# SwiGLU on two inner tiles at a time, and normed tiles kept in place

## The chip, the cores and the metric

The kernel runs on one core of one Trainium2 chip. The metric is device time of one execution in microseconds (us); the time of a kernel is the median of its runs. A profile comes from one further execution, whose span is taken from its first to its last instruction.

## What is computed

A decoder trunk of two layers for one sequence of 256 positions and 1024 features. Each layer has three sub-layers: a SwiGLU channel mixer (FFN), a sequence mixer (layer 0: a gated linear recurrence beside chunked linear attention; layer 1: latent attention), and a second FFN. Every sub-layer is modulated by a conditioning vector and closed by a norm over residual and output:

```python
D_MODEL = 1024; SEQ = 256; DEPTH = 2; D_FF = 2816

def layer_norm(x, g, b):
    xf = x.astype(F32)
    mu = jnp.mean(xf, -1, keepdims=True)
    var = jnp.mean(jnp.square(xf - mu), -1, keepdims=True)
    return ((xf - mu) * lax.rsqrt(var + LN_EPS) * g + b).astype(x.dtype)

def modulate(x, shift, scale):
    return x * (1 + scale[:, None, :]) + shift[:, None, :]

def deepnorm_residual(x, f, gate, g, b, weight=1.0):
    return layer_norm(DN_ALPHA * x + weight * (1 + gate[:, None, :]) * f, g, b)

def swiglu(u, w_in, w_out):
    gate, up = jnp.split(u @ w_in, 2, axis=-1)
    return (jax.nn.silu(gate) * up) @ w_out
```

## The kernel before, in words

**Layout.** Features lie on the 128 partitions, positions along the row: x is 8 tiles (k, or f on the output side) of 128x256. The inner width of an FFN is 22 tiles (j), each with a gate half and an up half.

**Weights.** All weights stream through in slabs of 16 tiles of 128x128 by one DMA each (SyncE's queue). Half a slab, 128x1024, is split at a time into a rounded high part (ScalarE, `whi`, L338) and the rest (VectorE, `wlo`, L339). `Stream.next` keeps three half slabs converted ahead, in four buffers. Now and then a conversion is followed on VectorE by one or two reductions of modulation weights (`junk`, L388).

**Products.** Values are held as a high and a low part as well. Each product of a 128x128 weight tile is three matmuls of 256 columns (`mm3`): high by high (L407), high weight by low value (L408), low weight by high value (L409).

**The FFN** (`ffn`). The first one, which starts while the modulation vectors are still being reduced, takes 8 inner tiles for k 0 to 3 and puts the sums aside (L725), then 8 others for all k, then the first 8 for k 4 to 7, with the sums added (L731). The other three have one early tile and a group of four. What is left is taken tile by tile (the tail). `glu` handles one inner tile: Silu of the gate on ScalarE (`sg`, L429), product with the up half on VectorE (`h`, L702), and the split into `hhi` (ScalarE, L444) and `hlo` (VectorE, L445). In a group the gate and the up half of one tile share a PSUM bank; in the tail each has a bank of its own.

**The boundary** (`Boundary`). `tile_out` adds an output tile to the residual `ax`, giving `y`; `stats` forms the mean and the variance with matmuls; `center` (L603) subtracts the mean tile by tile; `rsqrt2` yields `r` (L686, L687), which is minus twice the reciprocal deviation. While this goes on, TensorE multiplies the first tiles of the next sub-layer with values that are not yet normed (`early`), and two steps on VectorE correct the results (L641, L642). `u(k)` then makes the next input's tile k: `ut` = y times a column times r (VectorE, L657), `uhi` = ut plus a column, rounded (ScalarE, L658), `ulo` = the rest (VectorE, L659). `residual` makes `ax` for the next output: `xh` = y times a column times r (VectorE, L665), then ScalarE (L666) adds a column. There are six boundaries: the last ends the kernel; the one into the odd mixer (attention) has no `u` of its own but a residual; the other four have both. In the text they are counted from the first.

**Order.** Nothing is ordered by hand but the few steps around the statistics (`manual_schedule`). A list scheduler places each engine's instructions by priority (`high_priority`, with offsets UOFF for `u`, GOFF and GLATE for `glu`, EOFF for the early values). Once placed, each engine takes its list in order, so a step that waits holds up all that stand behind it.

Of the kernel before, what the change touches and what calls it, by code (L numbers as in the profile page):

```python
# [231 lines left out]
def trunk_kernel(ctx: ExitStack, tc: tile.TileContext, xT, cvec, pos, wst, modw, colsd,  # L232
# [281 lines left out]
    class Boundary:  # L514
# [79 lines left out]
        def stats(self, y, ysq):  # L594
# [7 lines left out]
            def center(k):  # L602
                vec.tensor_tensor(self.y[:, k, :], self.y[:, k, :], mean, SUB)  # L603

            odd_next = not self.last and self.next[1] == 1 and self.next[0] % 2
            with tc.high_priority(), tc.manual_schedule(engines={DVE, ACT}):
# [8 lines left out]
                for k in range(PRE):  # L615
                    center(k)
                r, rlast = rsqrt2(v, SEQ)
                self.r = r
                if self.last:
                    for k in range(KD):  # L620
                        self.normal(k, r)
                        if k + PRE < LPOOL:
                            center(k + PRE)
                    return
# [3 lines left out]
            self.center = center  # L628
# [15 lines left out]
            if odd_next:  # L644
                for k in range(PRE, KD):
                    center(k)

        def u(self, k):
# [4 lines left out]
            with tc.high_priority(offset=UOFF):  # L653
                if k >= PRE:
                    self.center(k)
                xa = T(wk, [P, SEQ], tag="ut")
                vec.scalar_tensor_tensor(xa, self.y[:, k, :], self.hA[:, k:k + 1], self.r, MULT, MULT)  # L657
                act.activation(uhi[:, k, :], xa, AF.Identity, bias=self.B[:, k:k + 1])  # L658
                vec.scalar_tensor_tensor(ulo[:, k, :], xa, self.B[:, k:k + 1], uhi[:, k, :].bitcast(F32), ADD, SUB)  # L659

        def residual(self, ks=range(KD)):
            W.pause = False
            for k in ks:
                xg = T(wk, [P, SEQ], tag="xh", bufs=3)
                vec.scalar_tensor_tensor(xg, self.y[:, k, :], self.ag[:, k:k + 1], self.r, MULT, MULT)  # L665
                act.activation(ax[:, k, :], xg, AF.Identity, bias=self.ab[:, k:k + 1])  # L666
# [24 lines left out]
    def ffn(l, i, prev):  # L691
        with tc.tile_pool(name=nm("ffn"), bufs=1) as fp:
# [4 lines left out]
            def glu(j, pg, pu, bg=0.0, bu=0.0, off=100):  # L697
                with tc.high_priority(offset=off):
                    sg = T(wk, [P, SEQ], tag="sg")
                    ta(sg, pg, AF.Silu, bias=bg)  # L700
                    h = T(wk, [P, SEQ], tag="h")
                    vec.scalar_tensor_tensor(h, pu, bu, sg, ADD, MULT)  # L702
                    split(h, hhi[:, j, :], hlo[:, j, :])

            for j in range(EARLY if prev else 0):
                (pg, bg), (pu, bu) = prev.values[2 * j:2 * j + 2]
                glu(j, pg, pu, bg, bu)

            passes = ffn_passes(l, i)
            part = {}  # L710
            for g, ks in passes:
                grp = {j: mmps() if q < 6 else axps() for q, j in enumerate(g)}
                for k in ks:
                    prev.u(k) if prev else first_u(k)
                    for j in g:
                        for half in range(2):
                            mm3(grp[j][:, half * SEQ:(half + 1) * SEQ], W.next((m, k, half * NJ + j)), u(k),
                                k == ks[0] and half == 0, k == ks[-1], True)
# [597 lines left out]
```

## Time and profile before

| | us |
|---|---|
| median of three runs | 1040.61 (1040.7, 1035.38, 1040.61) |
| profiled execution | 1033.83 |
| its span | 1032.1 |
| DVE busy, subtraction L339 alone | 416.7 |
| ACT busy, copy L338 alone | 357.6 |

The mean granted TensorE clock of the profiled execution was 0.996. PE is TensorE's matmuls, DVE VectorE, ACT ScalarE. A row of a group gives line, engine, operation, output and inputs with their shapes and the count, then busy us and mean ns, then idle time just before and what ended it. A row of a timeline gives start, duration and the operation, and in brackets the idle time before it and what ended that. Instructions of one engine overlap a little: the time that one holds up the queue is the distance to the next start.

### The profile page before, as it was taken

The numbers are of one execution on the slowest core, as the hardware profiler recorded it, in microseconds if no ns is written. First come the engines' busy times: TensorE is split into PE (matmuls) and PEld (weight loads), VectorE is DVE, ScalarE is ACT, GpSimd is POOL, SyncE is SP. The second block draws the span as 40 slices with busy tenths as digits, with TensorE's granted clock in tenths as the row PEclk, the third lists the DMA queues.
The fourth block names the chain that finished last, engine by engine and source line by source line (L and its number), as shares of the span: only waits on it lengthen the run. The fifth ranks groups of instructions, "written<-read, shape, count | busy, mean of one in ns | idle before, by whom it ended". The sixth has DMA issues, their size and how long they took to land.

```text
span 1032.1 us, 20703 instructions
## 1 busy us (share of the span) xinstructions
PE 995.5 (96%) x8338; PEld 972.8 (94%) x8338; DVE 884.7 (86%) x1491; ACT 612.5 (59%) x1023; POOL 54.8 (5%) x72
## 2 busy tenths in 40 slices
PE   6999999999999989999999999999999999999995
PEld 5999999998899979999999999999998889999995
DVE  5789999797998989999998899998888799666664
ACT  4746654567886656745545665455559666545543
POOL 0000010000001020000030000002000200000200
PEclk9999999999999999999999999999999999999998
DMA  9998798554466943699977469898743146665621
GB/s 342 366 339 319 257 368 309 208 204 169 170 264 242 350 185 142 245 361 373 365 279 286 166 251 371 322 359 321 286 167 129 73 164 245 246 224 187 243 83 41
DMA packets 38578, 258.57 MB, mean 251 GB/s; under 512 B 4289, under 2 KB 6849, under 8 KB 7762
## 3 DMA queue, kind: packets, MB, share of 16 engines
q1 hardware_dynamic: 38482, 257.25, 66.7%
q8 instruction: 65, 1.06, 0.4%
q14 instruction: 31, 0.25, 0.1%
HBM read 256.18 MB, written 1.05 MB: 249 GB/s over the span
## 4 chain that ended last, share of the span: by engine, by line
PE 82%; DVE 11%; issue 2%; ACT 2%; DMA 2%; POOL 0%; SPq 0%; DVEq 0%; ACTq 0%
PE mm L409 25%; PE mm L407 25%; PE mm L408 25%; DVE wlo L339 4%; DVE junk L388 2%; DMA wraw<-modw 1%; ACT whi L338 1%; DVE flat L557 1%; DVE yy L581 1%; PE ax L408 1%; PE ax L407 1%; PE ax L409 1%; DVE acc L589 1%; DVE flat L731 0%; DMA rgt<-rgw 0%
## 5 line engine op out<-in xcount | busy, mean ns | idle before, releaser
L339 DVE TENSOR_TENSOR wlo<-wraw,whi 128x1024 fp32r<-128x1024 f32 x340 | 416.7, 1233 | 81.3 <-ACT whi L338 80.8
L338 ACT ACTIVATE whi<-wraw 128x1024 fp32r<-128x1024 f32 x340 | 357.6, 1058 | 212.4 <-PE mm L408 138.0
L407 PE MATMUL mm<-uhi,whi 128*128 128x256 f32 x1672 | 461.4, 278 | 11.5 <-ACT uhi L444 6.0
L409 PE MATMUL mm<-uhi,wlo 128*128 128x256 f32 x1672 | 460.1, 277 | 3.6 <-DVE wlo L339 3.6
L408 PE MATMUL mm<-ulo,whi 128*128 128x256 f32 x1672 | 462.1, 277 | 0.7 <-DVE ulo L445 0.6
L407 PEld LDWEIGHTS mm<-uhi,whi 128*128 128x128 f32 x1672 | 313.6, 188 | 14.9 <-ACT uhi L444 7.9
L409 PEld LDWEIGHTS mm<-uhi,wlo 128*128 128x128 f32 x1672 | 313.8, 188 | 4.2 <-DVE wlo L339 4.1
L408 PEld LDWEIGHTS mm<-ulo,whi 128*128 128x128 f32 x1672 | 314.8, 188 | 1.5 <-DVE ulo L445 1.2
L409 PE MATMUL mm<-hhi,wlo 128*128 128x256 f32 x704 | 194.6, 276 | 1.9 <-DVE wlo L339 1.9
L408 PE MATMUL mm<-hlo,whi 128*128 128x256 f32 x704 | 194.4, 276 | 0.0
L407 PE MATMUL mm<-hhi,whi 128*128 128x256 f32 x704 | 194.3, 276 | 0.0
L388 DVE CUSTOM_DVE_ANT_0 junk<-wraw,cact,cols 128x1024 bf16<-128x1024 f32 x144 | 184.9, 1284 | 5.7 <-DMA wraw<-modw 5.0
L409 PEld LDWEIGHTS mm<-hhi,wlo 128*128 128x128 f32 x704 | 132.1, 188 | 2.3 <-DVE wlo L339 2.3
L407 PEld LDWEIGHTS mm<-hhi,whi 128*128 128x128 f32 x704 | 132.2, 188 | 0.0
L408 PEld LDWEIGHTS mm<-hlo,whi 128*128 128x128 f32 x704 | 132.2, 188 | 0.0
L571 POOL TENSOR_TENSOR ax<-ax,shift 128x256 f32<-128x256 f32 x42 | 42.2, 1039 | 734.7 <-ACT shift L569 734.7
L444 ACT ACTIVATE hhi<-h 128x256 fp32r<-128x256 f32 x88 | 35.9, 413 | 44.3 <-DVE h L702 43.2
L585 ACT ACTIVATE ysq<-yy 128x256 f32<-128x256 f32 x42 | 17.4, 414 | 51.8 <-DVE yy L581 50.0
L702 DVE SCALAR_TENSOR_TENSOR h<-mm,sg 128x256 f32<-128x256 f32 x75 | 30.9, 418 | 7.9 <-PE mm L409 7.9
L581 DVE SCALAR_TENSOR_TENSOR yy<-mm,gate,ax 128x256 f32<-128x256 f32 x48 | 22.8, 478 | 16.2 <-PE mm L409 15.0
L445 DVE TENSOR_TENSOR hlo<-h,hhi 128x256 fp32r<-128x256 f32 x88 | 36.0, 417 | 0.0
L429 ACT ACTIVATE sg<-mm 128x256 f32<-128x256 f32 x75 | 27.4, 366 | 3.0 <-DVE h L702 1.7
(288 smaller groups left out, 1088.1 us busy)
## 6 DMA issues: line engine op xcount, KB each, us to landing
wraw<-wst SPq DMA_DIRECT2D x169, 1024.0 KB, 5.8
wraw<-modw SPq DMA_DIRECT2D x71, 1024.0 KB, 6.5
wraw<-modw SPq DMA_DIRECT2D x2, 512.0 KB, 5.4
yy<-xT SPq DMA_DIRECT2D x8, 128.0 KB, 6.8
wraw<-wst SPq DMA_DIRECT2D x2, 512.0 KB, 7.9
rgt<-rgw SPq DMA_DIRECT2D x8, 128.0 KB, 3.7
outT<-yy SPq DMA_DIRECT2D x3, 256.0 KB, 2.6
outT<-yy SPq DMA_DIRECT2D x2, 128.0 KB, 2.6
```

The source lines that it names most:

```text
L338: act.activation(hi, raw, AF.Copy)
L339: i = vec.tensor_tensor(lo, raw, hi.bitcast(F32), SUB)
L388: i = vec.tensor_tensor_reduce(junk, t, cact, 1.0, col("mod_b", (l * NMOD + v) * KD + j), MULT, ADD, self.modcols[(l, v)][:, j:j + 1])
L407: pe.matmul(ps, hi, mh, start=start, stop=False, skip_group_check=shared)
L408: pe.matmul(ps, hi, ml, start=False, stop=False, skip_group_check=shared)
L409: pe.matmul(ps, lo, mh, start=False, stop=stop, skip_group_check=shared)
L429: i = act.activation(out, in_, func, **kw)
L444: act.activation(hi, src, AF.Copy)
L445: vec.tensor_tensor(lo, src, hi.bitcast(F32), SUB)
L571: pool.tensor_tensor(ax[:, j, :], ax[:, j, :], shift, SUB)
L581: vec.scalar_tensor_tensor(y, ps, self.gate[:, f:f + 1], ax[:, f, :], MULT, ADD)
L702: vec.scalar_tensor_tensor(h, pu, bu, sg, ADD, MULT)
```

## The change

It has four parts.

1. `glu` takes two inner tiles at once: the gates of a pair share one PSUM bank, the ups another, and Silu, product, rounding and subtraction run on 128x512. There are 41 pairs; the early tile and, in the three later FFNs, the last tile stay single. The product of a pair is a tensor_tensor. The order of the weight tiles, and so the matmuls' number and weights, stays.
2. `center` works on two tiles at a time, with the mean repeated by a broadcast, at all boundaries but the last.
3. A new step `normed` multiplies two tiles at a time by `r`, in place, so that `y` then holds the normed value. `u(k)` is made from it: `uhi` and the same value unrounded, `xa`, are both made on ScalarE (scale and bias as columns), and VectorE subtracts them (`ulo`, now a tensor_tensor). The first VectorE step of `u` is gone.
4. `residual` is one ScalarE step from the same normed value; its VectorE step is gone.

The new lines in the changed kernel: center L607, normed L610, mean copy L617, v L621, the early steps L652 and L653, uhi L673, xa L674, ulo L675, residual L680, rsqrt2 L701 and L702, the products of `glu` L719 (single) and L721 (pair), the added sums L759.

```diff
+            def wide(t, n):
+                return t[:, None, :].broadcast_to([P, n, SEQ])
+            def center(k, n=2):
+                vec.tensor_tensor(self.y[:, k:k + n, :], self.y[:, k:k + n, :], wide(mean, n), SUB)
+            def normed(k, n=2):
+                vec.tensor_tensor(self.y[:, k:k + n, :], self.y[:, k:k + n, :], wide(self.r, n), MULT)
...
             if odd_next:
-                for k in range(PRE, KD):
-                    center(k)
+                for k in range(0, KD, 2):
+                    if k >= PRE:
+                        center(k)
+                    normed(k)
...
             with tc.high_priority(offset=UOFF):
-                if k >= PRE:
-                    self.center(k)
+                if k % 2 == 0:
+                    if k >= PRE:
+                        self.center(k)
+                    self.normed(k)
+                z, a, b = self.y[:, k, :], self.hA[:, k:k + 1], self.B[:, k:k + 1]
                 xa = T(wk, [P, SEQ], tag="ut")
-                vec.scalar_tensor_tensor(xa, self.y[:, k, :], self.hA[:, k:k + 1], self.r, MULT, MULT)
-                act.activation(uhi[:, k, :], xa, AF.Identity, bias=self.B[:, k:k + 1])
-                vec.scalar_tensor_tensor(ulo[:, k, :], xa, self.B[:, k:k + 1], uhi[:, k, :].bitcast(F32), ADD, SUB)
+                act.activation(uhi[:, k, :], z, AF.Identity, bias=b, scale=a)
+                act.activation(xa, z, AF.Identity, bias=b, scale=a)
+                vec.tensor_tensor(ulo[:, k, :], xa, uhi[:, k, :].bitcast(F32), SUB)
...
-                xg = T(wk, [P, SEQ], tag="xh", bufs=3)
-                vec.scalar_tensor_tensor(xg, self.y[:, k, :], self.ag[:, k:k + 1], self.r, MULT, MULT)
-                act.activation(ax[:, k, :], xg, AF.Identity, bias=self.ab[:, k:k + 1])
+                act.activation(ax[:, k, :], self.y[:, k, :], AF.Identity, bias=self.ab[:, k:k + 1],
+                               scale=self.ag[:, k:k + 1])
...
-            def glu(j, pg, pu, bg=0.0, bu=0.0, off=100):
+            def glu(j, n, pg, pu, bg=0.0, bu=0.0, off=100):
                 with tc.high_priority(offset=off):
-                    sg = T(wk, [P, SEQ], tag="sg")
+                    sg = T(wk, [P, 2 * SEQ], tag="sg")[:, :n * SEQ]
                     ta(sg, pg, AF.Silu, bias=bg)
-                    h = T(wk, [P, SEQ], tag="h")
-                    vec.scalar_tensor_tensor(h, pu, bu, sg, ADD, MULT)
-                    split(h, hhi[:, j, :], hlo[:, j, :])
+                    h = T(wk, [P, 2 * SEQ], tag="h")[:, :n * SEQ]
+                    if n == 1:
+                        vec.scalar_tensor_tensor(h, pu, bu, sg, ADD, MULT)
+                    else:
+                        vec.tensor_tensor(h, pu, sg, MULT)
+                    split(h, *(t[:, j:j + n, :].rearrange("p j s -> p (j s)") for t in (hhi, hlo)))
...
-            for j in range(max(g.stop for g, _ in passes), NJ):
+            j = max(g.stop for g, _ in passes)
+            while j < NJ:
+                n = min(2, NJ - j)
                 pp = [mmps(), mmps()]
-                for half in range(2):
-                    for k in range(KD):
-                        mm3(pp[half][:, :SEQ], W.next((m, k, half * NJ + j)), u(k),
-                            k == 0, k == KD - 1)
-                glu(j, pp[0][:, :SEQ], pp[1][:, :SEQ])
+                for q in range(n):
+                    for half in range(2):
+                        for k in range(KD):
+                            mm3(pp[half][:, q * SEQ:(q + 1) * SEQ], W.next((m, k, half * NJ + j + q)), u(k),
+                                k == 0 and q == 0, k == KD - 1, True)
+                glu(j, n, *(ps[:, :n * SEQ] for ps in pp))
+                j += n
```

How the lists of the engines come out, at three places.

VectorE in the first FFN, where the last pass's products and the first tail products are split; `mod0` rows belong to the reduction before them. Before, between two conversions:

```order
L339 TENSOR_TENSOR wlo_248_1472<-wraw_202_1216,whi_247_1471 128x1024
L702 SCALAR_TENSOR_TENSOR h_227_1360<-flat1_90_464,sg_226_1358 128x256
L702 SCALAR_TENSOR_TENSOR h_240_1433<-mm_229_1365,sg_239_1431 128x256
L388 ISA junk_249_1475,mod0_3_236_1402<-wraw_201_1214,cact_5_96,cols_6_97 128x1024
L388 ISA mod0_3_236_1402 128x1
L445 TENSOR_TENSOR hlo_31_145<-h_240_1433,hhi_30_144 128x256
L445 TENSOR_TENSOR hlo_31_145<-h_227_1360,hhi_30_144 128x256
L702 SCALAR_TENSOR_TENSOR h_252_1505<-mm_242_1438,sg_251_1503 128x256
L388 ISA junk_250_1477,mod0_3_236_1402<-wraw_201_1214,cact_5_96,cols_6_97 128x1024
L388 ISA mod0_3_236_1402 128x1
L702 SCALAR_TENSOR_TENSOR h_261_1571<-mm_254_1510,sg_260_1569 128x256
L445 TENSOR_TENSOR hlo_31_145<-h_252_1505,hhi_30_144 128x256
```

And now, at the same place:

```order
L339 TENSOR_TENSOR wlo_224_1384<-wraw_186_1128,whi_223_1383 128x1024
L388 ISA junk_222_1357,mod0_3_220_1354<-wraw_185_1126,cact_5_96,cols_6_97 128x1024
L388 ISA mod0_3_220_1354 128x1
L721 TENSOR_TENSOR h_211_1312<-flat1_90_464,sg_210_1310 128x512
L721 TENSOR_TENSOR h_232_1449<-mm_213_1317,sg_231_1447 128x512
L339 TENSOR_TENSOR wlo_228_1416<-wraw_194_1192,whi_227_1415 128x1024
L445 TENSOR_TENSOR hlo_31_145<-h_232_1449,hhi_30_144 128x512
L445 TENSOR_TENSOR hlo_31_145<-h_211_1312,hhi_30_144 128x512
L388 ISA junk_229_1419,mod0_3_220_1354<-wraw_193_1190,cact_5_96,cols_6_97 128x1024
L388 ISA mod0_3_220_1354 128x1
L339 TENSOR_TENSOR wlo_236_1456<-wraw_194_1192,whi_235_1455 128x1024
```

Four products and three splits became two and two of double width, and the two reductions no longer stand in one stretch between conversions.

VectorE in the even mixer, where the recurrence (`ya`, L843 to L853, with L853 the scans) and the attention's decays (`bc`, `lb`) are formed. Before:

```order
L665 SCALAR_TENSOR_TENSOR xh_513_3248<-yy_299_1821,ag_314_1849,r_401_2597 128x256
L968 TENSOR_TENSOR lb_457_2980<-lb_457_2980,mm_514_3251 128x256
L843 SCALAR_TENSOR_TENSOR ya1_495_3168<-xh_512_3228,ya1_495_3168 128x256
L665 SCALAR_TENSOR_TENSOR xh_517_3282<-yy_299_1821,ag_314_1849,r_401_2597 128x256
L844 TENSOR_SCALAR ya2_496_3169<-ya2_496_3169 128x1024
L665 SCALAR_TENSOR_TENSOR xh_523_3320<-yy_299_1821,ag_314_1849,r_401_2597 128x256
L845 SCALAR_TENSOR_TENSOR ya2_496_3169<-ya1_495_3168,ya2_496_3169 128x1024
L967 TENSOR_TENSOR bc_458_2981<-bc_458_2981,mm_518_3285 128x256
L846 SCALAR_TENSOR_TENSOR ya2_496_3169<-ya2_496_3169 128x1024
L339 TENSOR_TENSOR wlo_522_3291<-wraw_480_3075,whi_521_3290 128x1024
```

And now, with lines higher by 32:

```order
L1000 TENSOR_TENSOR lb_429_2908<-lb_429_2908,mm_485_3177 128x256
L875 SCALAR_TENSOR_TENSOR ya1_467_3096<-xh_484_3156,ya1_467_3096 128x256
L876 TENSOR_SCALAR ya2_468_3097<-ya2_468_3097 128x1024
L877 SCALAR_TENSOR_TENSOR ya2_468_3097<-ya1_467_3096,ya2_468_3097 128x1024
L999 TENSOR_TENSOR bc_430_2909<-bc_430_2909,mm_488_3209 128x256
L878 SCALAR_TENSOR_TENSOR ya2_468_3097<-ya2_468_3097 128x1024
L339 TENSOR_TENSOR wlo_492_3215<-wraw_452_3003,whi_491_3214 128x1024
```

The three steps of the residual are gone from between the others, whose order is kept.

The third boundary, between layer 0's second FFN and layer 1's first, on VectorE. Before, from `r` on:

```order
L687 SCALAR_TENSOR_TENSOR r_1143_7301<-t_1144_7302,r_1143_7301 128x256
L339 TENSOR_TENSOR wlo_1149_7317<-wraw_1119_7089,whi_1148_7316 128x1024
L657 SCALAR_TENSOR_TENSOR ut_1145_7309<-yy_1042_6526,hA_1048_6537,r_1143_7301 128x256
L641 SCALAR_TENSOR_TENSOR early_1151_7346<-mean_1142_7294,wab_1150_7344,mm_1146_7313 128x256
L657 SCALAR_TENSOR_TENSOR ut_1170_7431<-yy_1042_6526,hA_1048_6537,r_1143_7301 128x256
L659 SCALAR_TENSOR_TENSOR ulo_18_124<-ut_1145_7309,B_1045_6529,uhi_17_123 128x256
L642 SCALAR_TENSOR_TENSOR early_1151_7346<-early_1151_7346,r_1143_7301 128x256
```

And now:

```order
L702 SCALAR_TENSOR_TENSOR r_1063_7119<-t_1064_7120,r_1063_7119 128x256
L339 TENSOR_TENSOR wlo_1069_7136<-wraw_1039_6909,whi_1068_7135 128x1024
L610 TENSOR_TENSOR yy_962_6346<-yy_962_6346,r_1063_7119 128x512
L652 SCALAR_TENSOR_TENSOR early_1071_7165<-mean_1062_7114,wab_1070_7163,mm_1066_7132 128x256
L610 TENSOR_TENSOR yy_962_6346<-yy_962_6346,r_1063_7119 128x512
L653 SCALAR_TENSOR_TENSOR early_1071_7165<-early_1071_7165,r_1063_7119 128x256
L675 TENSOR_TENSOR ulo_18_124<-ut_1065_7128,uhi_17_123 128x256
```

Two normed pairs stand where two single steps stood, and both early steps now come ahead of the first `ulo`. The same place on ScalarE, before:

```order
L658 ACTIVATE uhi_17_123<-ut_1145_7309,B_1045_6529 128x256
L338 ACTIVATE whi_1168_7403<-wraw_1126_7155 128x1024
L429 ACTIVATE sg_1160_7389<-early_1151_7346,wab_1150_7344 128x256
L658 ACTIVATE uhi_17_123<-ut_1170_7431,B_1045_6529 128x256
L639 ACTIVATE wab_1155_7378<-mm_1152_7349 128x2
```

And now:

```order
L673 ACTIVATE uhi_17_123<-yy_962_6346,B_965_6349,hA_968_6357 128x256
L674 ACTIVATE ut_1065_7128<-yy_962_6346,B_965_6349,hA_968_6357 128x256
L673 ACTIVATE uhi_17_123<-yy_962_6346,B_965_6349,hA_968_6357 128x256
L429 ACTIVATE sg_1080_7208<-early_1071_7165,wab_1070_7163 128x256
L674 ACTIVATE ut_1090_7250<-yy_962_6346,B_965_6349,hA_968_6357 128x256
L650 ACTIVATE wab_1075_7197<-mm_1072_7168 128x2
L673 ACTIVATE uhi_17_123<-yy_962_6346,B_965_6349,hA_968_6357 128x256
L674 ACTIVATE ut_1093_7283<-yy_962_6346,B_965_6349,hA_968_6357 128x256
L673 ACTIVATE uhi_17_123<-yy_962_6346,B_965_6349,hA_968_6357 128x256
L674 ACTIVATE ut_1098_7319<-yy_962_6346,B_965_6349,hA_968_6357 128x256
L338 ACTIVATE whi_1088_7222<-wraw_1046_6975 128x1024
```

The weight copy that followed the first `uhi` now follows the fourth.

More of the change, by code (lines that the diff above doesn't have):

```diff
@@ L614, in stats @@
                 vec.tensor_tensor(v, e2, v, SUB)
-                for k in range(PRE):
-                    center(k)
+                if self.last:
+                    for k in range(PRE):
+                        center(k, 1)
+                else:
+                    for k in range(0, PRE, 2):
+                        center(k)
                 r, rlast = rsqrt2(v, SEQ)
@@ L622, in stats @@
                         if k + PRE < LPOOL:
[L623 removed]
+                            center(k + PRE, 1)
                     return
@@ L627, in stats @@
                 W.pause = PAUSE
-            self.center = center
+            self.center, self.normed = center, normed
             if not odd_next:
```

43 lines of the change are left out of this document (25 added, 18 removed).

## Prediction

> **What bounds the kernel now.** I read the page's first part, then the windows, then the waits of the matmul queue, and then the timeline around each of those waits.
>
> ```profile
> span 1032.1 us, 20703 instructions
> PE 995.5 (96%) x8338; PEld 972.8 (94%) x8338; DVE 884.7 (86%) x1491; ACT 612.5 (59%) x1023; POOL 54.8 (5%) x72
> ```
>
> TensorE is busy for 96% of the span. The change leaves its matmuls and the weight tiles as they are, so nothing can be won but in the 4% where it waits. Stretches of 20 us (columns: PE, PEld, DVE, ACT, POOL, each busy us with its count) show where VectorE is the fuller of the two:
>
> ```profile
> 100.00:120.00 20.00, 20.00 (x179) 20.00 (x178) 20.00 (x36) 13.55 (x25) 0.00 (x0) 1.00 0.74 275
> 120.00:140.00 20.00, 18.96 (x167) 18.76 (x166) 20.00 (x33) 12.46 (x20) 0.00 (x0) 1.00 0.90 333
> 260.00:280.00 20.00, 17.48 (x149) 17.04 (x148) 19.63 (x30) 16.61 (x28) 2.40 (x1) 1.00 0.43 158
> 583.00:605.00 22.00, 22.00 (x196) 22.00 (x195) 21.96 (x40) 13.66 (x23) 0.00 (x0) 1.00 0.51 186
> ```
>
> 179 matmuls in 20 us are one per 0.112 us, the undisturbed pace. In the first row VectorE has no gap at all, and TensorE still runs at full pace on the slabs converted ahead; in the second and third VectorE is as full and TensorE loses time. The waits of the matmul queue (us in all, times, longest):
>
> ```profile
> PE mm L409 <- DVE wlo L339: 6.5, 6, 1.5
> ...
> PE mm L408 <- DVE ulo L445: 0.6, 1, 0.6
> PE mm L1167 <- DVE e L1159: 0.5, 1, 0.5
> ```
>
> So of 36 us without a matmul only 6.5 + 0.6 + 0.5 = 7.6 us end on VectorE work that this change makes lighter or shifts. The list has no wait for a PSUM bank. That 7.6 us is the most that the change can give.
>
> **The change part by part.** Durations of the groups that it touches, or that resemble the new ones:
>
> ```profile
> L445 DVE TENSOR_TENSOR hlo<-h,hhi 128x256 fp32r<-128x256 f32 x88 | 36.0, 417 | 0.0
> L665 DVE SCALAR_TENSOR_TENSOR xh<-yy,ag,r 128x256 f32<-128x256 f32 x40 | 17.9, 475 | 0.0
> L657 DVE SCALAR_TENSOR_TENSOR ut<-yy,hA,r 128x256 f32<-128x256 f32 x32 | 15.2, 476 | 0.0
> L731 DVE TENSOR_TENSOR flat<-mm,flat 128x512 f32<-128x512 f32 x6 | 4.0, 681 | 0.0
> L658 ACT ACTIVATE uhi<-ut,B 128x256 fp32r<-128x256 f32 x32 | 16.0, 505 | 9.3 <-DVE ut L657 8.9
> L509 ACT ACTIVATE ut<-yy,mod,scp 128x256 f32<-128x256 f32 x8 | 4.8, 599 | 18.2 <-DVE scp L507 18.2
> ```
>
> Alone, a 128x512 operation takes 681 ns against 2 x 417 = 834, so a merge saves 153 ns. In a queue that is never empty neighbours overlap, and the start of the next row counts. Such a stretch, in the first FFN's tail, on VectorE, and the matmul that it holds up:
>
> ```profile
> 117.11 0.42 DVE L445 TENSOR_TENSOR hlo<-h,hhi 128x256 fp32r<-128x256 f32 x1
> 117.45 0.68 DVE L731 TENSOR_TENSOR flat<-ax,flat 128x512 f32<-128x512 f32 x1
> 118.05 1.21 DVE L339 TENSOR_TENSOR wlo<-wraw,whi 128x1024 fp32r<-128x1024 f32 x1
> ...
> 119.85 1.27 DVE L388 CUSTOM_DVE_ANT_0 junk<-wraw,cact,cols 128x1024 bf16<-128x1024 f32 x1
> ...
> 122.06 1.27 DVE L388 CUSTOM_DVE_ANT_0 junk<-wraw,cact,cols 128x1024 bf16<-128x1024 f32 x1
> ...
> 123.93 1.22 DVE L339 TENSOR_TENSOR wlo<-wraw,whi 128x1024 fp32r<-128x1024 f32 x1
> ```
> ```profile
> 125.20 0.38 PE L409 MATMUL mm<-uhi,wlo 128*128 128x256 f32 x1 [1.04 <-DVE wlo L339]
> ```
>
> From 117.11 to 117.45 a 256-wide operation holds the queue 0.34 us, from 117.45 to 118.05 a 512-wide one 0.60: a merge in a full queue saves 0.07 us.
>
> *Product and split, pairs, first FFN.* Eleven pairs merge 22 operations on VectorE: 22 x 0.07 = 1.5 us of relief over 90 us, which by itself moves little. The Trainium skill ("VectorE: DVE Perf Modes", section "The TRN2 errata — SBUF-src ops pay a fixed extra latency per instruction") gives an fp32 tensor_tensor (N+151)/0.96 ns and advises tiles of 512 elements and more, since the fixed part is paid once; that is 157 ns a merge and an estimated 3.5 us here, which would make the sum below 2.0 us lower. The single rows agree with it to a few ns (153 against 157), the queued rows do not. What counts more is the order. Before, two reductions, four products and three splits stand between the subtraction at 118.05 and the one at 123.93, which ends 1.04 us late for the matmul at 125.20. In the changed order one reduction, two double products or two double splits stand between neighbouring subtractions, so the late one comes over a microsecond earlier: -1.2 us (1.04, and the slower pace of the matmul after it). The two later waits of this stretch stay: the reductions before them are as many. Bounds: 0, and -2.9 us, what the stage's three waits amount to:
>
> ```profile
> PE mm L409 <- DVE wlo L339: 2.9, 3, 1.2
> ```
>
> *Residual without VectorE.* Forty L665 go (17.9 us), each 0.40 us in a full queue. They are worth time only where TensorE waits behind them, and this is the even mixer, VectorE first, then TensorE:
>
> ```profile
> 262.18 0.48 DVE L665 SCALAR_TENSOR_TENSOR xh<-yy,ag,r 128x256 f32<-128x256 f32 x1
> ...
> 270.56 3.31 DVE L339 TENSOR_TENSOR wlo<-wraw,whi 128x1024 fp32r<-128x1024 f32 x1
> ...
> 276.79 0.47 DVE L665 SCALAR_TENSOR_TENSOR xh<-yy,ag,r 128x256 f32<-128x256 f32 x1
> 277.18 1.21 DVE L339 TENSOR_TENSOR wlo<-wraw,whi 128x1024 fp32r<-128x1024 f32 x1
> ```
> ```profile
> 273.93 0.38 PE L409 MATMUL mm<-uhi,wlo 128*128 128x256 f32 x1 [1.02 <-DVE wlo L339]
> ...
> 278.45 0.38 PE L409 MATMUL mm<-uhi,wlo 128*128 128x256 f32 x1 [1.50 <-DVE wlo L339]
> ```
>
> Three L665 stand ahead of the first late subtraction and a fourth ahead of the second (277.18 - 276.79 = 0.39 each), in a queue that hardly pauses from 258 on. The first comes 1.2 us earlier and its wait of 1.02 us goes; the second comes 1.6 us earlier, but TensorE is there 1.2 us earlier too, and 0.4 us of its 1.50 goes: -1.6 us. Bounds: 0 (if the queue then waits for the scan's inputs) and -2.5, both waits. In the odd mixer one L665 and a subtraction stand ahead of the softmax products for which L1167 waits 0.5 us: -0.4 us, bounds 0 and -0.5. The scaling moves to ScalarE, 599 ns instead of 505; no matmul waits for the residual until the next sub-layer's output.
>
> *The next input at a boundary.* This is where the change adds. Third boundary, VectorE, ScalarE and TensorE in turn:
>
> ```profile
> 580.66 0.42 DVE L687 SCALAR_TENSOR_TENSOR r<-t,r 128x256 f32<-128x256 f32 x1
> 581.00 1.22 DVE L339 TENSOR_TENSOR wlo<-wraw,whi 128x1024 fp32r<-128x1024 f32 x1
> 582.13 0.48 DVE L657 SCALAR_TENSOR_TENSOR ut<-yy,hA,r 128x256 f32<-128x256 f32 x1
> ...
> 583.32 0.48 DVE L659 SCALAR_TENSOR_TENSOR ulo<-ut,B,uhi 128x256 fp32r<-128x256 f32 x1
> ```
> ```profile
> 582.65 0.51 ACT L658 ACTIVATE uhi<-ut,B 128x256 fp32r<-128x256 f32 x1 [0.47 <-DVE ut L657]
> 583.81 1.06 ACT L338 ACTIVATE whi<-wraw 128x1024 fp32r<-128x1024 f32 x1 [0.66 <-PE mm L408]
> ```
> ```profile
> 583.73 0.64 PE L407 MATMUL mm<-uhi,whi 128*128 128x256 f32 x4
> 584.21 0.28 PE L408 MATMUL mm<-ulo,whi 128*128 128x256 f32 x1
> ```
>
> Before, ulo of the first k is ready at 583.80 and first read at 584.21: 0.41 us to spare. After, r is 0.14 us later (the last mean-subtraction between t and r is a pair, 0.60 for 0.34; the two pairs ahead of t pay back 0.14 of that). Then subtraction L339, normed pair 0 from 582.27, the early value 582.87, normed pair 1 583.26, the other early step 583.86, ulo 584.19 to 584.60. Both activations are done by then (uhi 582.95 to 583.55, xa to 584.1). TensorE starts its first four L407 on time, then misses ulo by 0.4 to 0.5 us. I take 0.45 at three boundaries, which are alike. At the second, before, ulo stands ahead of a subtraction:
>
> ```profile
> 401.39 0.48 DVE L659 SCALAR_TENSOR_TENSOR ulo<-ut,B,uhi 128x256 fp32r<-128x256 f32 x1
> 401.79 1.22 DVE L339 TENSOR_TENSOR wlo<-wraw,whi 128x1024 fp32r<-128x1024 f32 x1
> ```
> ```profile
> 401.92 0.39 PE L408 MATMUL mm<-ulo,whi 128*128 128x256 f32 x1
> ```
>
> In the changed order the normed pair (0.60 for 0.40) and the subtraction (1.13 to the next start) come first, two other steps no longer do (L657 of the second k, 0.40); ulo begins about 0.93 us later, at 402.32, ends at 402.74, and the matmul of 401.92 is 0.9 us late. Cost: 3 x 0.45 + 0.9 = +2.25 us. Bounds: +1.4 (r not later, so 0.25 each and 0.7), and +4.5 (1.13 each, if a subtraction stands ahead everywhere). The fourth boundary, into the odd mixer, has neither uhi nor ulo and costs nothing.
>
> What waits behind the new work: on ScalarE the second activations and the residual stand ahead of the weight copy that began at 583.81 and now begins near 587.5, after the activations of three more k. With four buffers it is needed three half slabs of 24 matmuls on, 583.73 + 3 x 2.7 = 591.8; copy and subtraction end near 589.8. I cost that at nothing: 2 us cover it. The shared banks I cost at nothing as well: a pair's products start 6 matmuls (0.7 us) later than its first tile's did, but the waits above show no wait for a bank, and the last pair of an FFN (four operations of 0.6 to 0.7 us, 2.6 us) is read only as the 21st of 22 inner tiles, 20 x 0.34 = 6.7 us into the output product.
>
> **Sum.** -1.2 - 1.6 - 0.4 + 2.25 = -0.95 us. The profiled execution took 1033.83 us, its span 1032.1, so 1032.9 for it. The three runs gave 1040.7, 1035.38 and 1040.61: the profiled one lies by the fastest. The median of 1040.61 becomes 1039.6. A measurement of this kernel can tell about 0.5%, 5.2 us, from no change.
>
> **Rivals.** *The relief pays in full* (0.17). VectorE loses about 36 of 885 us (L657 15.2 and L665 17.9 go, 20 normed pairs of 0.68 come, the merges give the rest); with that slack every wait for wlo, 6.5 us, goes, and the boundary's extra steps find gaps. For it: all six waits are on one line, in full stretches. Against it: the order at the boundaries is fixed, TensorE is there with 0.4 us to spare, and the reductions stay in the first FFN. Time: 1040.6 - 6.5 = 1034.1, faster.
>
> *ScalarE's weight copies come late* (0.13), the one that ends on the other side. Per k of a first pass (2.7 us) ScalarE has one copy of 1.06, two activations of 0.5 to 0.6 and, later, a residual of 0.6: 2.7 to 2.9 us, less what neighbours overlap. From the point where that exceeds 2.7, or the 2 us of cover are used up by the activations moved ahead, TensorE waits at each boundary for a copy and its subtraction, 1.06 + 1.23 = 2.3 us. Four boundaries: +9.2; with the sum's gains kept, 1040.6 - 0.95 + 9.2 = 1048.9, slower; with half of them late 1044.3. Against it: ScalarE is busy for 13.66 us of the 22 from 583 on, and eight more activations of 0.5 to 0.6 make 18.
>
> *The change does not do what it says* (0.15): merging gives nothing in full queues and the late subtraction of the first FFN stays late, for instance behind reductions. Then the sum lacks 1.2: +0.25, 1040.9, no change.
>
> **How the numbers follow.** The forecast has 0.55. Its own bounds are -5.9 + 1.4 = -4.5 and 0 + 4.5, so 1036.1 to 1045.1, and I leave 0.02 and 0.01 of its chance beyond 5.2 us on either side for what I have not seen. Faster: 0.17 + 0.02 = 0.19. Slower: 0.13 + 0.01 = 0.14. The same: 0.67. The range takes in the first rival at its 1034.1 and the half case of the second with a microsecond beyond each: 1033 to 1046.
>
> **What would show it.** Right: the waits for wlo near 124 and 272 gone, that near 278 at about 1.1 us; a new wait of L408 for ulo at four places, 2.25 us in all; VectorE's busy time down by some 36 us and TensorE's first and last matmul hardly moved. Wrong towards faster: no wait for ulo at all. Wrong towards slower: waits of L407 for whi or of L409 for wlo some 8 us behind a boundary, or matmuls that wait for a product to leave a bank.

## The result and the profile after

The changed kernel takes 1053.72 us (median of six runs, 1051.42 to 1054.19) against 1037.45 for before (six runs, 1033.61 to 1040.7). The ratio is 1.0159, with a 95% interval of 1.0133 to 1.0184: slower by about 16 us, outside the forecast range. (The prediction started from 1040.61, the median of the first three of these runs of before.) The profiled execution has a span of 1051.8 us, 19.7 more than before's.

The page's first part, after:

```profile
span 1051.8 us, 20412 instructions
PE 1006.5 (96%) x8338; PEld 981.6 (93%) x8338; DVE 862.6 (82%) x1337; ACT 620.8 (59%) x973; POOL 55.1 (5%) x72
```

VectorE was relieved by 22 us, and the kernel still became longer. The waits of the matmul queue after (us in all, times, longest):

```profile
PE mm L409 <- DVE wlo L339: 7.5, 10, 1.4
PE ax L566 <- ACT shift L564: 6.7, 2, 4.4
...
PE mm L407 <- ACT whi L338: 1.8, 2, 1.4
...
PE mm L408 <- DVE ulo L675: 1.0, 3, 0.4
```

The second row is new: twice, at the start of an FFN's output product, TensorE waits for the shift that ScalarE makes of the first output tile; before's list has no wait there. The waits of VectorE itself show where that comes from. Before:

```profile
DVE junk L388 <- DMA wraw<-modw: 5.0, 6, 1.3
```

And after:

```profile
DVE junk L388 <- DMA wraw<-modw: 36.3, 25, 3.6
```

VectorE stands idle for 36.3 us in front of reductions of modulation weights whose data have not landed. Matching the n-th matmul of the two traces (there are 8338 in each) shows where the time is lost:

| n-th matmul | before, us | after, us | after later by |
|---|---|---|---|
| 4050 (end of the second FFN's input) | 515.1 | 517.1 | 2.0 |
| 4200 (start of its output) | 532.1 | 538.4 | 6.3 |
| 5250 (third FFN) | 652.6 | 659.5 | 6.9 |
| 5700 | 703.6 | 715.2 | 11.6 |
| 5850 (start of its output) | 720.6 | 739.2 | 18.6 |
| 8250 (last FFN) | 1009.8 | 1029.4 | 19.7 |

So some 16 of the 19.7 us are lost in the tails of two FFNs, the second and third, and at the first tile of their outputs. In those two FFNs half of the reductions run, 72 of 144. The 4.7 us between matmuls 5250 and 5700 are lost at stalls of up to 1.0 us in the third FFN's tail. The list of waits after, from 655 to 745 us, puts 2.2 us of them down to the subtraction; before, from 640 to 730, has no wait at all:

```profile
PE mm L409 <- DVE wlo L339: 2.2, 4, 0.8
```

In both lists VectorE has the same 144 reductions and the same 340 weight subtractions (L339), but their order differs. Before, around the first output tile of the second FFN, VectorE:

```profile
521.24 1.22 DVE L339 TENSOR_TENSOR wlo<-wraw,whi 128x1024 fp32r<-128x1024 f32 x1
522.67 1.23 DVE L339 TENSOR_TENSOR wlo<-wraw,whi 128x1024 fp32r<-128x1024 f32 x1 [0.21 <-ACT whi L338]
523.81 0.48 DVE L581 SCALAR_TENSOR_TENSOR yy<-mm,gate,ax 128x256 f32<-128x256 f32 x1
524.21 1.27 DVE L388 CUSTOM_DVE_ANT_0 junk<-wraw,cact,cols 128x1024 bf16<-128x1024 f32 x1
```

After, the same place:

```profile
527.47 1.28 DVE L388 CUSTOM_DVE_ANT_0 junk<-wraw,cact,cols 128x1024 bf16<-128x1024 f32 x1 [0.88 <-DMA wraw<-modw]
...
528.80 1.28 DVE L388 CUSTOM_DVE_ANT_0 junk<-wraw,cact,cols 128x1024 bf16<-128x1024 f32 x1
...
530.01 1.22 DVE L339 TENSOR_TENSOR wlo<-wraw,whi 128x1024 fp32r<-128x1024 f32 x1
531.15 0.48 DVE L581 SCALAR_TENSOR_TENSOR yy<-mm,gate,ax 128x256 f32<-128x256 f32 x1
```

A pair of reductions now stands in front of a subtraction and of the output tile's addition (L581), where it stood behind them. The weights of that pair were asked for on SyncE's queue at 519.95, and the chain of waits after gives the time on the way:

```profile
519.95 7.39 DMA wraw<-modw
```

They land near 527.3, and the pair, the subtraction and the addition follow. In before the same pair was asked for at 515.77 and its turn on VectorE came at 524.21, 8.4 us later:

```profile
515.77 0.33 SPq L372 DMA_DIRECT2D wraw<-modw  x1
```

After, its turn comes 7.5 us behind the request, and the request itself goes out 4.2 us later than before: in the chain it follows the subtraction that ends at 519.93, while TensorE is only some 2 us behind by then. Over the 36 pairs of the two FFNs the median time from the request to the start of the pair's first reduction is 8.9 us before and 7.0 us after. So in this chain VectorE's waits also hold up the subtractions, and with them the next requests.

The matmul that needs the shifted tile comes only then, where before it did not wait; the same happens at the third FFN's output. The second FFN's before, then both after:

```profile
527.56 0.28 PE L566 MATMUL ax<-shift,ones_r 128*128 128x256 f32 x1
```
```profile
532.13 0.55 PE L566 MATMUL ax<-shift,ones_r 128*128 128x256 f32 x1 [2.39 <-ACT shift L564]
```
```profile
726.40 0.38 PE L566 MATMUL ax<-shift,ones_r 128*128 128x256 f32 x1 [4.36 <-ACT shift L564]
```

Each of the two waits costs more than its length, since the granted clock falls behind it. Windows after (PE busy, clock ahead of the last two columns):

```profile
526.00:532.00 6.00, 3.74 (x34) 1.00 0.96 356
532.00:536.00 4.00, 3.87 (x19) 0.57 0.98 350
536.00:540.00 4.00, 4.00 (x37) 1.00 0.35 139
...
726.00:730.00 4.00, 3.60 (x18) 0.59 0.96 385
```

In 4 us TensorE starts 18 or 19 matmuls in place of 37; against starts 0.113 us apart that adds up to 1.5 and 1.7 us more, on top of the waits.

### The profile page after: what moved, and what is told of

Read it like the earlier page. It is cut to its first block, busy times and chain, and to the rows that moved or that the text cites. A ratio compares the mean times of both kernels' runs of the same rounds, so it can differ in the third digit from the quotient of the medians.

```text
span 1051.8 us, 20412 instructions
## 1 busy us (share of the span) xinstructions
PE 1006.5 (96%) x8338; PEld 981.6 (93%) x8338; DVE 862.6 (82%) x1337; ACT 620.8 (59%) x973; POOL 55.1 (5%) x72
## 3 DMA queue, kind: packets, MB, share of 16 engines
q8 instruction: 65, 1.06, 0.4%
## 4 chain that ended last, share of the span: by engine, by line
PE 67%; DVE 15%; DMA 8%; issue 5%; ACT 3%; POOL 0%; DVEq 0%; SPq 0%; ACTq 0%
PE mm L408 20%; PE mm L409 20%; PE mm L407 20%; DMA wraw<-modw 8%; DVE wlo L339 5%; DVE junk L388 3%; ACT whi L338 1%; DVE hlo L445 1%; PE mm L1018 1%; PE mm L1017 1%; PE mm L1019 1%; DVE h L721 1%; PE ax L408 1%; DVE yy L581 1%; PE ax L409 1%
## 5 line engine op out<-in xcount | busy, mean ns | idle before, releaser
L339 DVE TENSOR_TENSOR wlo<-wraw,whi 128x1024 fp32r<-128x1024 f32 x340 | 415.3, 1232 | 92.6 <-ACT whi L338 90.4
L407 PE MATMUL mm<-uhi,whi 128*128 128x256 f32 x1672 | 462.1, 279 | 10.8 <-ACT uhi L444 5.4
L407 PEld LDWEIGHTS mm<-uhi,whi 128*128 128x128 f32 x1672 | 314.5, 189 | 14.0 <-ACT uhi L444 7.3
L388 DVE CUSTOM_DVE_ANT_0 junk<-wraw,cact,cols 128x1024 bf16<-128x1024 f32 x144 | 185.4, 1287 | 37.5 <-DMA wraw<-modw 36.3
L407 PE MATMUL mm<-hhi,whi 128*128 128x256 f32 x704 | 195.8, 278 | 0.0
L407 PEld LDWEIGHTS mm<-hhi,whi 128*128 128x128 f32 x704 | 133.7, 190 | 0.0
L444 ACT ACTIVATE hhi<-h 128x512 fp32r<-128x512 f32 (+1 forms) x47 | 28.1, 601 | 75.5 <-DVE h L721 71.0
L581 DVE SCALAR_TENSOR_TENSOR yy<-mm,gate,ax 128x256 f32<-128x256 f32 x48 | 22.9, 479 | 17.7 <-PE mm L409 16.5
L445 DVE TENSOR_TENSOR hlo<-h,hhi 128x512 fp32r<-128x512 f32 (+1 forms) x47 | 30.2, 650 | 0.0
L407 PE MATMUL mm<-flat,whi 128*128 128x258 f32 x96 | 29.0, 302 | 0.0
L408 PE MATMUL mm<-flat,whi 128*128 128x258 f32 x96 | 29.0, 302 | 0.0
```

The source lines that it names most:

```text
L339: i = vec.tensor_tensor(lo, raw, hi.bitcast(F32), SUB)
L388: i = vec.tensor_tensor_reduce(junk, t, cact, 1.0, col("mod_b", (l * NMOD + v) * KD + j), MULT, ADD, self.modcols[(l, v)][:, j:j + 1])
L407: pe.matmul(ps, hi, mh, start=start, stop=False, skip_group_check=shared)
L408: pe.matmul(ps, hi, ml, start=False, stop=False, skip_group_check=shared)
L444: act.activation(hi, src, AF.Copy)
L445: vec.tensor_tensor(lo, src, hi.bitcast(F32), SUB)
```

## The experiments

**Theory A**: the changed list puts the reductions of the second and third FFN two subtractions (in the mean) earlier than before, so that they stand in front of urgent work before their data land, and VectorE, which takes its list in order, waits. **Theory B**: products of pairs come late, at the end of an FFN or because of the shared banks. **Theory C**: the second activations delay the weight copies on ScalarE. In the table, *lead* is by how many weight subtractions the 72 reductions of these two FFNs stand earlier than before, in the mean, from the lists; *idle* is VectorE's idle time ahead of reductions until a landing, in the profiled execution; before itself has 5.0 us. Each ratio is to runs of before taken beside that kernel, whose medians lie between 1035.67 and 1037.45.

| kernel | lead | idle, us | median, us | ratio to before, interval |
|---|---|---|---|---|
| changed | 1.96 | 36.3 | 1053.72 | 1.0159 (1.0133 to 1.0184) |
| pinned | -0.07 | 1.4 | 1036.39 | 0.9997 (0.9983 to 1.0011) |
| pairs only | 0.25 | 4.7 | 1035.54 | 0.9988 (0.9971 to 1.0004) |
| normed only | 2.12 | 32.9 | 1048.79 | 1.0120 (1.0092 to 1.0147) |
| before, early reductions | 1.96 | 22.0 | 1053.89 | 1.0165 (1.0138 to 1.0192) |
| resident data | 1.96 | 2.7 | 1036.52 | 1.0017 (1.0004 to 1.0029) |
| lead of one | 1.00 | 25.7 | 1041.20 | 1.0042 (1.0023 to 1.0060) |
| first k as before | -0.07 | 3.1 | 1034.97 | 1.0000 (0.9986 to 1.0014) |
| one later | -0.92 | 1.0 | 1035.76 | 0.9996 (0.9984 to 1.0009) |
| xa on VectorE | 1.06 | 31.9 | 1041.59 | 1.0047 (1.0026 to 1.0069) |
| xa and residual on VectorE | 0.36 | 10.6 | 1037.01 | 1.0017 (0.9998 to 1.0037) |

**Pinned.** Each reduction is tied to the subtraction behind which it stood before.

```diff
+    PIN = [...]   # subtractions ahead of the i-th reduction, before the change
...
+                self.los.append(i)
...
+            n = PIN[self.nred]
+            self.nred += 1
+            if n:
+                queue_behind(i, self.los[n - 1])
```

> The changed kernel, with each reduction of modulation weights tied on VectorE behind the weight subtraction that it followed before the change (within one subtraction). Theory A (in the changed list the reductions of the second and third FFN stand two to four subtractions earlier than before, ahead of the landing of their weights, and hold up VectorE): VectorE's idle time before reductions falls from 36 us to under 10, the two waits of TensorE for the shift at the start of an output product (2.4 and 4.4 us) go, and the kernel takes 1036 to 1041 us. Theory B (products of pairs are finished late, at the end of an FFN and for the shared banks): still 1050 or more. Theory C (the second activations delay the weight copies on ScalarE): still 1048 or more.

The whole loss is gone, with all four parts of the change in place. VectorE's wait before reductions, and the waits of the matmul queue (lines are higher by 4 and 9 than in the changed kernel):

```profile
DVE junk L393 <- DMA wraw<-modw: 1.4, 3, 0.8
```
```profile
PE mm L418 <- DVE wlo L343: 4.6, 4, 1.4
...
PE mm L417 <- DVE ulo L684: 1.3, 4, 0.4
...
PE ax L575 <- ACT shift L573: 0.3, 1, 0.3
```

That refutes B and C as the cause of the 16 us.

**Pairs only, and normed only.** The change in two halves: part 1 alone, and parts 2 to 4 alone. In words, since each is made of the matching parts of the change's diff:

```text
 pairs only:  glu(j, n, ...), shared banks, the tail in pairs; center, u, residual as before
 normed only: center in pairs, normed, u, residual as changed; glu(j, ...) on single tiles
```

> Only the pairs of inner tiles, with their shared banks; mean subtraction, next input and residual as before. The reductions stand where they stood before, within one subtraction. Theory A: 1034 to 1038 us, no new wait for reductions. Theory B: 1048 or more. Theory C: as before, 1037.

> Only the normed tiles: mean subtraction in pairs, normed pairs, next input with two activations, residual in one; products tile by tile as before. The reductions stand where the changed kernel has them, two to four subtractions early. Theory A: 1050 to 1056 us, with some 30 us of VectorE idle before reductions. Theory B: at most 1041. Theory C: 1048 or more as well, but with TensorE waiting for the weight copy (L407 for whi), not for what stands behind a reduction.

Pairs cost nothing and, within the interval, bring nothing. The loss is in the other half. Its waits are those of A, not of C: 32.9 us before reductions, and L407 for `whi` has 2.0 us, where before had 2.2. It took 1048.79, just under A's 1050: 1.2% of the 1.6%. The two intervals overlap, so whether the pairs, which cost nothing alone, add the rest on top of it is not shown.

**Before, with early reductions.** The converse of pinned: nothing of the change, but 72 reductions where the changed kernel has them.

```diff
+    EARLIER = [...]   # subtractions ahead of the i-th reduction, after the change; 999: as it comes
...
+                while self.todo and EARLIER[self.nred] <= s:
+                    ahead = self.reduce()
...
+                if ahead is not None:
+                    queue_behind(i, ahead)
...
```

> The kernel before, with nothing changed but the place of 72 reductions (second and third FFN): each stands on VectorE where the changed kernel has it, two to four subtractions earlier. Theory A: 1047 to 1055 us, with over 25 us of VectorE idle before reductions. Theories B and C: within 3 us of before, as neither pairs nor second activations are in it.

The place of the reductions alone makes before's kernel as slow as the changed one, with less idle time than expected, 22.0 us in place of over 25. Here the wait of TensorE appears at another line: L424 is the product with the low weight part, L346 the subtraction.

```profile
DVE junk L398 <- DMA wraw<-modw: 22.0, 16, 3.1
```
```profile
PE mm L424 <- DVE wlo L346: 16.3, 15, 2.6
```

**Resident data.** The changed kernel's order, held by the same list, but those 72 reductions do not read what is brought for them.

```diff
-            i = vec.tensor_tensor_reduce(junk, t, cact, 1.0, ...)
+            i = vec.tensor_tensor_reduce(junk, cact if EARLIER[self.nred] < 999 else t, cact, 1.0, ...)
```

> The changed kernel in its own order, each reduction where it stands there; but the 72 reductions of the second and third FFN read a tile that is always in memory in place of the weights that are brought for them, which are still brought and then overwritten unread (so later modulation values are not the reference's, and the buffer of those weights comes free at their landing). Theory A, waiting for the landing: no idle time before reductions, and 1034 to 1040 us. The rival within it, that the reductions' own 1.3 us in front of urgent subtractions are what costs: 1046 or more, with TensorE still waiting for wlo in the tails of those FFNs.

With the reductions in the same places and of the same length, all of the loss but 0.2% is gone: 1.0017. So it is the wait for the landing that costs, not the 1.3 us that a reduction takes in front of a subtraction. One thing differs besides: the buffer of the modulation weights comes free at its landing and not at its reduction, which also lets later transfers start sooner (the pair asked for at 519.95 in the changed kernel is asked for at 511.69 here). How much goes by the missing wait and how much by the earlier transfers, this run does not tell; the place in the list by itself costs no more than the 0.2% in either case.

**Lead of one.** The changed kernel with every one of the 72 held one subtraction earlier than before (the list of the kernel with early reductions, with other numbers).

```diff
-    EARLIER = [...]   # as after the change
+    EARLIER = [...]   # one less than before the change
```

> The changed kernel with the 72 reductions of the second and third FFN held one subtraction earlier than they stood before the change (the changed kernel has them 2.0 earlier in the mean, pinned has them at 0). If the loss grows with the lead over the landing: between the two, 1039 to 1047 us, with 8 to 20 us of VectorE idle before reductions. If only a few far-moved reductions cost: within 2 us of pinned, 1034 to 1038.

1041.2 us, 25.7 us of idle time (more than the 8 to 20 expected): of that idle time about a fifth comes through to the end. The loss grows faster than the lead: 0.4% at one, 1.6% at two.

**The first k as before.** Pinned, and at each boundary the first k of the next input on the old way.

```diff
-                if k % 2 == 0:
+                if k == 0:
+                    xa = T(wk, [P, SEQ], tag="ut")
+                    vec.scalar_tensor_tensor(xa, self.y[:, k, :], self.hA[:, k:k + 1], self.r, MULT, MULT)
+                    act.activation(uhi[:, k, :], xa, AF.Identity, bias=self.B[:, k:k + 1])
+                    vec.scalar_tensor_tensor(ulo[:, k, :], xa, self.B[:, k:k + 1], uhi[:, k, :].bitcast(F32), ADD, SUB)
+                    return
+                if k == 1:
+                    self.normed(0)
+                elif k % 2 == 0:
...
```

> Pinned, and the first k of each boundary's next input made as before the change (scaled and multiplied by r in one step on VectorE, one activation, one subtraction with the column), the normed pair only behind it. Against pinned the waits of L408 for ulo at the four boundaries (1.3 us in its profile, 2.7 us in the matmuls' positions) should go: 1033.5 to 1035.5 us, ratio to before 0.997 to 0.999. If those waits are hidden anyway: as pinned, 1036.

The waits for `ulo` fall as meant, from four of 1.3 us in all in pinned to

```profile
PE mm L417 <- DVE ulo L692: 0.4, 1, 0.4
```

but the time cannot be told from before or from pinned: the ratio is 1.0000, not 0.997 to 0.999. What it wins lies under the scatter of the runs.

**One later.** The same, with the reductions held one subtraction later where the program's order allows.

```diff
-    PIN = [...]   # as before the change
+    PIN = [...]   # one more, at most the place at which the program issues it
```

> As the kernel with the first k as before, but the reductions of the second and third FFN held one subtraction later than before the change, where the program's order allows it. Where the landing decides: some of the remaining 5 us of VectorE idle before reductions goes, and 0 to 1 us of time; where the reductions' late end delays the next sub-layer's columns: 1 to 5 us slower than with the first k as before.

0.9996: no change. Idle time before reductions is down to 1.0 us, and the list of waits has none for a sub-layer's columns. The kernel cannot be told from before or from pinned.

**Which step moves the reductions.** Two variants of the changed kernel with nothing held: first `xa` is made on VectorE again, then the residual's scaling too.

```diff
-                act.activation(xa, z, AF.Identity, bias=b, scale=a)
+                vec.tensor_scalar(xa, z, a, b, MULT, ADD)
...
+                vec.tensor_scalar(xg, self.y[:, k, :], self.ag[:, k:k + 1], None, MULT)
+                act.activation(ax[:, k, :], xg, AF.Identity, bias=self.ab[:, k:k + 1])
-                act.activation(ax[:, k, :], self.y[:, k, :], AF.Identity, bias=self.ab[:, k:k + 1],
-                               scale=self.ag[:, k:k + 1])
```

> The changed kernel with nothing held in place; only xa is made on VectorE (one operation with the two columns) in place of the second activation. In its list the 72 reductions stand 1.1 subtractions earlier than before the change in the mean, where the changed kernel has 2.0. Theory A, by the lead: about as the kernel with a lead of one, 1039 to 1045 us. If the second activation itself is what costs: 1037 or less.

> As the one before, and the residual's scaling too on VectorE (from the normed tile, then one activation with the column). Mean lead 0.4 subtractions. Theory A: 1035 to 1039 us, 5 to 12 us of VectorE idle before reductions, though VectorE has more to do than in the changed kernel.

Putting work back on VectorE makes the kernel faster: 1041.6, then 1037.0 us. The lead falls with it, from 1.96 to 1.06 and 0.36, and the time follows the lead as in the pinned kernels: a lead of 1.06 that came about in this way costs 0.47%, a lead of 1.00 set by hand 0.42%.

## Why the prediction was wrong

**The step that failed** is the account of what is moved. The prediction followed the change at three places, the first FFN, the even mixer and a boundary, and costed there what stands in front of what. For the reductions it said only that in the first FFN "the reductions before them are as many", and that they "stay in the first FFN". For the second and third FFN it had no term at all, and gave no reason for leaving them out. But the list of an engine is made anew: the half of the change that takes two operations per tile off VectorE, and puts a second activation on ScalarE, lets the scheduler place the 72 reductions of those two FFNs two subtractions sooner, ahead of their data. In place of nothing that cost 16 us: VectorE's idle time ahead of reductions went from 5.0 to 36.3 us, holding the reductions in their old places brought the ratio back to 0.9997, and moving them alone gave 1.0165. The two variants above show that the two steps move them; by which of its rules the scheduler does so, no run here shows.

The order of the whole list was at hand before the run. Counting, for each reduction, how many subtractions precede it would have shown the shift of two, and before's page has 6.5 us as the median time from the request of such a transfer to its landing. That would have raised the question; the price of the shift does not follow from these two numbers alone.

**The sum itself**, which the pinned kernel tests alone, is not contradicted: -0.95 us forecast, ratio 0.9997 (-0.3 us, interval -1.8 to +1.1). That is in part luck, since several terms were off and terms that it did not have made up for them. The two profiled executions differ by +2.4 us, since each is one draw (last section). Term by term, by matching the matmuls of pinned and before:

- First FFN, -1.2 us: the wait near 124 is gone, and TensorE gains 1.35 us there. But behind it a wait of 1.40 us is new (at 161.08), the one of 1.21 us grew to 1.41, and the one of 0.68 us is gone; by the end of the stage the gain is 0.1 us. The statement that those two stay was wrong, and so was its ground: ahead of the subtraction that the new wait ends on two reductions stand (156.81 and 158.13), where one stood before (157.53).
- Even mixer, -1.6: -0.7. The two waits shrank from 1.02 and 1.50 us to 0.71 and 1.12. The first late subtraction starts at 270.52, where it started at 270.56 before, and TensorE is 0.3 us later by then; so the three steps that are gone bring 0.3 us and not 1.2, in part since VectorE then waits 0.55 us for an activation, the kind of wait that the prediction's zero bound had. The second wait comes out at the 1.1 us that the prediction named, but by luck: it had TensorE 1.2 us ahead there. The changed kernel shows the same, its subtraction 0.8 us and TensorE 0.45 us earlier than before:

```profile
263.22 0.70 DVE L876 TENSOR_SCALAR ya<-ya 128x1024 f32<-128x1024 f32 x1 [0.55 <-ACT ya L429]
...
269.76 3.32 DVE L339 TENSOR_TENSOR wlo<-wraw,whi 128x1024 fp32r<-128x1024 f32 x1
```

- Odd mixer, -0.4: -0.3. The wait for the softmax products is gone; one of 0.4 us, for a value of ScalarE (`ovt`), is new.
- Boundaries, +2.25: +2.7 (0.6, 0.9, 0.6 and 0.6). The mechanism was right to the row. At the third boundary, pinned (VectorE, then TensorE):

```profile
583.79 0.68 DVE L619 TENSOR_TENSOR yy<-yy,r 128x512 f32<-128x512 f32 x1
584.39 0.47 DVE L661 SCALAR_TENSOR_TENSOR early<-mean,wab,mm 128x256 f32<-128x256 f32 x1
584.78 0.69 DVE L619 TENSOR_TENSOR yy<-yy,r 128x512 f32<-128x512 f32 x1
585.38 0.42 DVE L662 SCALAR_TENSOR_TENSOR early<-early,r 128x256 f32<-128x256 f32 x1
585.72 0.42 DVE L684 TENSOR_TENSOR ulo<-ut,uhi 128x256 fp32r<-128x256 f32 x1
```
```profile
586.19 0.39 PE L417 MATMUL mm<-ulo,whi 128*128 128x256 f32 x1 [0.30 <-DVE ulo L684]
```

  From the first normed pair to the start of `ulo` 1.92 us were forecast, 1.93 measured; of the matmul's 0.6 us delay the wait is 0.30 in its own row, the rest a slower start of it and of the matmuls behind it.
- Not foreseen: the wait of 1.06 us near 350, for a subtraction, is gone (-1.35); near 282 there is a new one of 0.67 us for a VectorE product in the even mixer (`la`), and by 300 the 0.7 us won in that mixer are lost again; between 375 and 390 TensorE loses 1.6 us more than before, with its clock (last section).
- Costed at nothing: rightly, the shared banks (pairs only, 0.9988) and the weight copies moved behind three more k (L407 for `whi` waits 1.8 us, before 2.2).

**The rivals.** That the relief pays in full did not happen: VectorE lost 22 us of busy time, not 36 (by the prediction's own prices for a full queue, 72 steps of 0.40 less, 20 of 0.60 more and 102 merges of 0.07, it comes to 24), and the waits for `wlo` fell in pinned from 6.5 to 4.6 us only. The slower rival had the right sign, but its cause, late copies on ScalarE, was not the one.

## What to carry to other kernels

When a scheduler makes the order, taking work off an engine also moves the work that stays: compare the whole list of that engine, and for every instruction that waits for a transfer count what it now precedes. An in-order engine should not meet such an instruction before the data can be there; tie it behind the work that covers its landing, here one line per reduction, before judging the rest of the change. And price work off the critical path at what waits for it: 22 us less of VectorE were worth nothing measurable here.

## What was not expected of the hardware

The same wait costs different amounts behind it. In the even mixer's output TensorE has gaps of 1.47 and then 2.20 us between starts in before, 1.44 and 2.18 us in pinned. Behind the second gap pinned has 15 starts at about half pace (0.21 us apart in place of 0.113), some 1.6 us of delay; in before only the first start behind each gap is slow. A window behind the second gap shows it, before first (PE busy, PEld, DVE, ACT, POOL, clock):

```profile
385.00:389.00 4.00, 2.93 (x25) 2.93 (x26) 4.00 (x8) 1.44 (x4) 0.00 (x0) 1.00 0.00 0
```
```profile
385.00:389.00 4.00, 3.67 (x22) 3.67 (x23) 3.61 (x6) 0.82 (x2) 0.00 (x0) 0.71 0.00 0
```

The clock is 1.00 in the one and 0.71 in the other, though the matmuls and, to 0.03 us, the gaps are the same. The changed kernel's execution even has before's gaps, 1.47 and 2.20 us, and its clock falls to half from 385.42 on.

The clock records of the traces show what differs. In the twelve executions (before, changed and the ten experiments) the clock falls to half 17 times between its first rise and the last matmul. Each time it stays there for 3.41 us, and each time it begins a whole number of 3.41 us after that rise. So each execution has a raster of its own. In 13 of the raster's stretches no matmul ran for 1.9 us or more, and the half clock followed every one of them. In before the second gap, from 383.87 to 386.07, lies across a border of the raster at 385.28, and neither of the two stretches has more than 1.2 us of it; in pinned nearly all of it lies in one stretch, from 383.29 to 386.70. Three of the other four half-clock stretches follow 1.4 to 1.6 us without a matmul, though other stretches with 1.4 to 1.8 us had no such consequence; the fourth (pairs only, at 234) follows none, and why is open.

The Trainium skill ("TensorE: Matmul & The Clock Gate", section "Part 1: The HAM clock gate (the "warmup" mystery)") describes a monitor that halves the clock after an idle window of about 3.4 us, counted in windows that run on their own and not from the start of a wait. The halving, the length and the raster of its own agree with these records; that 1.9 us without a matmul within such a window are enough is less than the idle window that it states, and here the measurement decides. Where a gap falls on the raster is luck from one execution to the next. One such stretch costs some 1.6 us, and it makes up most of the 2.4 us between the two profiled executions; the terms above are no more exact than that.
